# Seven half-size block products for 20 tile pairs of the first channel-mixing product, with weight sums on GpSimd

## Chip, cores and metric

The kernel runs on one NeuronCore of a Trainium2 chip. The metric is the device time of one execution in microseconds. TensorE is the matmul engine, VectorE (DVE), ScalarE (ACT) and GpSimd (POOL) compute beside it, and SyncE (SP) issues most DMAs.

## What is computed

One decoder block on 512 tokens of width 1024: a mixing sub-layer (a recurrence and a dilated attention, merged by gates) and a channel sub-layer. The change lies in the channel sub-layer:

```python
h = modulate(rms_norm(x, g_pre_ffn[i]), shift_f, scale_f)
u, gt = jnp.split(h @ w_ffn_in[i], 2, axis=-1)
f = (jax.nn.silu(u) * gt) @ w_ffn_out[i]
x = x + gate_f[:, None, :] * rms_norm(f, g_post_ffn[i])
```

The products are wanted nearly in fp32. Every operand is therefore split into a rounded part (hi) and a residual (lo), and every block product is three matmuls: hi x hi, hi x lo, lo x hi.

## The kernel before

A helper `split` (L110 to L112) casts a tile to its high part on ScalarE (L111) and subtracts it on VectorE for the residual (L112). `weights(i)` loads one weight tile of 128x1024 fp32 (512 KB) on SP's queue into one of three slots called raw, and splits it; the high and low tiles have two slots each in the pool wp, or come from another pool that is passed in. `mm3` issues the three matmuls of a block. All this is traced at high priority, so that a scheduler puts it ahead of the work that is traced beside it, in each engine's queue; within a queue the order is then fixed.

The end of the kernel, in order. **Merge**: eight channel tiles of the merged mixers, split into mh and ml. **Output product** (`natural_gemm`, tokens on the partitions): eight k tiles; the first four are taken for all four token tiles in turn, the last four ("tail") are held back and taken token tile by token tile, so that each tile's accumulation ends as early as possible. **Norm** (`post_norm`, and the lines behind it): for each token tile the residual x2 and the normalised row xn. After two token tiles their rows are transposed on TensorE (L915), evacuated with scale and shift (hf, L921 and L923) and split into h2h and h2l, 256 columns at a time.

**First channel-mixing product**: 22 pairs of weight tiles, u (for SiLU) and g. For a tile, eight k blocks of 128x128 are multiplied with h2 over all 512 tokens: `ffn_mm`, 24 matmuls of 512 columns. The first two pairs are computed in token halves (256 columns) while the second half of h2 is still being made; their weights lie in wp and in the pool ow. The other 20 pairs follow. For each pair `ffn_evac` applies SiLU (L945), multiplies by g (L946) and splits the result into fh and fl for the second product. After pair 8 the last eight columns of the modulation (`ada_col`, a weight tile times the condition vector on VectorE, L168) are loaded on POOL's queue and `ada_comb` forms comb_f. **Second channel-mixing product**: `natural_gemm` over 22 k tiles, with the norm and the output behind it.

There are eight PSUM banks of 512 columns, in four groups that rotate: mm (3), b (2), c (2), y (1). A pair now takes two banks of mm.

Of the kernel before, what the change touches and what calls it, by code (L numbers as in the profile page):

```python
# [18 lines left out]
P = 128  # L19
D = 1024  # L20
# [64 lines left out]
def block_kernel(ctx, tc, x, vec, cst, cst2, cst3, crow, ada, win0, lora, wts, wa, out):  # L85
# [21 lines left out]
    def mm(o, l, r, start, stop):  # L107
        return nc.tensor.matmul(o, l, r, start=start, stop=stop)  # L108

    def split(hi, lo, src):  # L110
        A.copy(hi, src)  # L111
        V.tensor_tensor(out=lo, in0=src, in1=r32(hi), op=ALU.subtract)  # L112

    def weights(i, pool=None, src=None, n=1024):
        with tc.high_priority():
            raw = wp.tile([P, 1024], F32, tag="raw", name=nm("raw"), bufs=3)[:, 0:n]
            nc.sync.dma_start(raw, wts[i] if src is None else src)
            if pool is None:
# [43 lines left out]
        V.reciprocal(t, t)  # L162
        return t

    def ada_col(pool, tag, bufs, i, eng):
        aw = pool.tile([P, D], F32, tag=tag, name=nm("aw"), bufs=bufs)
# [671 lines left out]
    with ExitStack() as phY:  # L838
        yp = phY.enter_context(tc.tile_pool(name="yp", bufs=1))
        for ct in range(KT):  # L840
# [11 lines left out]
            V.tensor_tensor(out=gb, in0=gb, in1=ya, op=ALU.add)  # L852
            split(mh[:, ct, :], ml[:, ct, :], gb)
    phZ.close()
    phH = ExitStack()
    h2p = phH.enter_context(tc.tile_pool(name="h2p", bufs=1, side="right"))
    h2h = h2p.tile([P, KT, S], F32R, name="h2h")
    h2l = h2p.tile([P, KT, S], F32R, name="h2l")

    op_ = phO.enter_context(tc.tile_pool(name="op", bufs=1))  # L860
    op_.tile([P, 80], F32, name="pad_o")
    ow = phO.enter_context(tc.tile_pool(name="ow", bufs=6))

    def natural_gemm(w0, nk, ah, al, tail, pool):
        accs = [[bank("mm"), bank("mm")], [bank("mm"), bank("c")], [bank("c"), bank("y")], [bank("b"), bank("b")]]

        def part(k, wh, wl, i, hs=(0, 1)):
            t = slice(i * P, (i + 1) * P)
            for (l, w, first, last) in ((ah, wh, True, False), (al, wh, False, False), (ah, wl, False, True)):
                for h in hs:  # L870
                    mm(accs[i][h], l[:, k, t], w[:, h * 512:(h + 1) * 512], k == 0 and first, k == nk - 1 and last)
        for k in range(nk - tail):
            wh, wl = weights(w0 + k)
            for i in range(NTT):
                part(k, wh, wl, i)
# [24 lines left out]
    xns = []  # L900
    for i, acc in natural_gemm(W_OUT, KT, mh, ml, 4, ow):
        post_norm(op_, acc, comb_m, x2[i], x2[i])
        s1 = op_.tile([P, 1], F32, tag="s1", name=nm("s1"), bufs=2)
        xn = op_.tile([P, D], F32, tag="xn", name=nm("xn"), bufs=2)
        A.activation(xn, x2[i], AF.Square, accum_out=s1)
        rs = rstd_of(op_, s1, D, 1, eps_rms)
        V.tensor_scalar(out=xn, in0=x2[i], scalar1=rs, scalar2=None, op0=ALU.mult)
        xns.append(xn)
        if i % 2 == 1:
            t0 = (i - 1) * P  # L910
            for j2 in range(KT // 2):
                pt = bank("c" if i == 1 else "b")
                for jj in range(2):
                    for ii in range(2):
                        nc.tensor.transpose(pt[:, (2 * jj + ii) * P:(2 * jj + ii + 1) * P],  # L915
                                            xns[i - 1 + ii][:, (2 * j2 + jj) * P:(2 * j2 + jj + 1) * P], ident)
                for jj in range(2):
                    j = 2 * j2 + jj
                    hf = op_.tile([P, 256], F32, tag="hf2", name=nm("hf2"), bufs=2)
                    if jj == 0:  # L920
                        A.activation(hf, pt[:, 0:256], AF.Identity, scale=modf[:, 8 + j:9 + j], bias=modf[:, j:j + 1])  # L921
                    else:
                        V.tensor_scalar(out=hf, in0=pt[:, 256:512], scalar1=modf[:, 8 + j:9 + j], scalar2=modf[:, j:j + 1], op0=ALU.mult, op1=ALU.add)  # L923
# [133 lines left out]
```

## Time and profile before

| | us |
|---|---|
| median of 3 runs | 995.48 |
| lowest and highest | 989.5, 1003.88 |
| profiled execution | 990.31 |
| span from first to last instruction of it | 988.5 |
| TensorE busy (matmul) | 945.8, 96% |
| VectorE busy | 577.2, 58% |
| ScalarE busy | 396.1, 40% |
| GpSimd busy | 41.9, 4% |

The mean granted clock of TensorE is 0.98 of full speed. The profile puts a group's count, busy time, the mean of one, and the idle time of its engine in front of it side by side; a timeline row has a start, a length and what the engine waited for. Matmuls overlap: one of 512 columns shows 0.39 us, but the next starts sooner, so a stream is read from the starts.

### The profile page before, as it was taken

Reading aid. Unit: us, or ns where it says so; the run is one execution under the profiler, and the core shown is the slowest. Engines: PE = TensorE matmul, PEld = TensorE weight load, DVE = VectorE, ACT = ScalarE, POOL = GpSimd, SP = SyncE. Lnnn points to the kernel's source line nnn. Section 1 sums busy time; section 2 is a strip of 40 time slices with the busy share of each in tenths; the row PEclk is TensorE's granted clock in tenths of the full one; section 3 lists DMA queues with packets and bytes.
Section 4 is the critical chain, followed back from the end, with each engine's and each line's share of the span. In section 5 each row is a group of like instructions: output and inputs, shape, how many; then the busy total and the mean of one; then the engine's idle time right before and its main releaser. Section 6 shows DMA issues by size and latency. Waiting matters only on the chain.

```text
span 988.5 us, 13834 instructions
## 1 busy us (share of the span) xinstructions
PE 945.8 (96%) x5468; PEld 757.5 (77%) x5468; DVE 577.2 (58%) x1050; ACT 396.1 (40%) x633; POOL 41.9 (4%) x85
## 2 busy tenths in 40 slices
PE   6999989999999999998999899999999999999997
PEld 4887767777867876786788678988888888888885
DVE  6986799955699975375655576573333333412234
ACT  7568443433586232332382246532323232321223
POOL 0000000100010010010000100010000000000000
PEclk9999999999999987999899999999999999999999
DMA  9753435423231322139326863163332323233322
GB/s 369 280 164 117 157 122 173 136 97 116 100 125 63 102 91 86 34 139 277 122 93 219 292 223 96 42 232 97 99 119 95 106 87 107 86 107 89 103 86 86
DMA packets 47170, 131.73 MB, mean 133 GB/s; under 512 B 11249, under 2 KB 12033, under 8 KB 47106
## 3 DMA queue, kind: packets, MB, share of 16 engines
q1 hardware_dynamic: 27792, 96.74, 30.0%
q10 hardware_dynamic: 13970, 16.27, 5.2%
q0 software_dynamic: 5344, 17.84, 4.8%
q8 instruction: 43, 0.70, 0.3%
q14 instruction: 21, 0.17, 0.1%
HBM read 116.14 MB, written 14.69 MB: 132 GB/s over the span
## 4 chain that ended last, share of the span: by engine, by line
PE 74%; DVE 10%; issue 8%; DMA 5%; ACT 2%; ACTq 1%; POOL 0%; SPq 0%; DVEq 0%; POOLq 0%
PE ps L108 72%; DVE lo L112 1%; DVE fP L526 1%; DMA k<-d_k 1%; DVE fT L530 1%; DMA d_ya<-t 1%; DMA aw<-in_ada_dram 1%; DVE T L534 1%; DMA x<-in_x_dram 1%; DMA gb<-d_gate 1%; ACT xg L490 1%; DVE aw L168 1%; PE ps L308 1%; DVE Sg L486 0%; DMA VN<-d_v 0%
## 5 line engine op out<-in xcount | busy, mean ns | idle before, releaser
L111 ACT CAST hi<-raw 128x1024 fp32r<-128x1024 f32 (+1 forms) x130 | 133.0, 1025 | 346.0 <-PE ps L108 276.0
L112 DVE TENSOR_TENSOR lo<-raw,hi 128x1024 fp32r<-128x1024 f32 (+1 forms) x130 | 154.6, 1189 | 167.6 <-ACT hi L111 161.6
L108 PE MATMUL ps<-hl,hi 128*128 128x512 f32 x432 | 175.1, 405 | 0.0
L108 PE MATMUL ps<-hh,lo 128*128 128x512 f32 x432 | 174.3, 403 | 0.8 <-DVE lo L112 0.8
L108 PE MATMUL ps<-hh,hi 128*128 128x512 f32 x432 | 172.7, 409 | 0.2
L108 PE MATMUL ps<-h2h,hi 128*128 128x512 f32 (+1 forms) x352 | 133.5, 381 | 0.7 <-ACT u L945 0.7
L108 PE MATMUL ps<-h2l,hi 128*128 128x512 f32 (+1 forms) x352 | 133.5, 380 | 0.2 <-DVE h2l L112 0.2
L108 PE MATMUL ps<-h2h,lo 128*128 128x512 f32 (+1 forms) x352 | 133.2, 379 | 0.0
L108 PEld LDWEIGHTS ps<-hh,lo 128*128 128x128 f32 x432 | 82.8, 192 | 18.5 <-DVE lo L112 1.2
L108 PEld LDWEIGHTS ps<-hh,hi 128*128 128x128 f32 x432 | 82.6, 191 | 18.6 <-issue 1.3
L108 PEld LDWEIGHTS ps<-hl,hi 128*128 128x128 f32 x432 | 82.9, 192 | 16.7 <-issue 0.2
L108 PEld LDWEIGHTS ps<-h2h,hi 128*128 128x128 f32 x352 | 66.0, 188 | 13.7 <-ACT u L945 0.9
L108 PEld LDWEIGHTS ps<-h2l,hi 128*128 128x128 f32 x352 | 66.1, 188 | 13.1 <-DVE h2l L112 0.4
L108 PEld LDWEIGHTS ps<-h2h,lo 128*128 128x128 f32 x352 | 66.1, 188 | 12.5
L168 DVE SCALAR_TENSOR_TENSOR aw<-aw,silur 128x1024 f32<-128x1024 f32 x48 | 58.2, 1219 | 9.4 <-DMA aw<-in_ada_dram 9.3
L946 DVE TENSOR_TENSOR u<-u,ps 128x512 f32<-128x512 f32 x22 | 15.0, 687 | 66.6 <-PE ps L108 59.0
L108 PE MATMUL ps<-hi,fh 128*128 128x512 f32 x144 | 44.4, 389 | 0.0
L108 PE MATMUL ps<-lo,fh 128*128 128x512 f32 x144 | 44.4, 389 | 0.0
L108 PE MATMUL ps<-hi,fl 128*128 128x512 f32 x144 | 44.3, 389 | 0.0
L108 PEld LDWEIGHTS ps<-hi,fh 128*128 128x128 f32 x144 | 27.0, 188 | 5.7
L108 PEld LDWEIGHTS ps<-hi,fl 128*128 128x128 f32 x144 | 27.0, 188 | 5.6
L108 PEld LDWEIGHTS ps<-lo,fh 128*128 128x128 f32 x144 | 27.0, 188 | 5.6
(292 smaller groups left out, 1372.9 us busy)
## 6 DMA issues: line engine op xcount, KB each, us to landing
raw<-in_wts_dram SPq DMA_DIRECT2D x124, 512.0 KB, 3.6
aw<-in_ada_dram SPq DMA_DIRECT2D x40, 512.0 KB, 4.3
d_gate<-t POOLq DMA_DIRECT2D x16, 256.0 KB, 3.0
aw<-in_ada_dram POOLq DMA_DIRECT2D x8, 512.0 KB, 4.7
raw<-in_win_dram SPq DMA_DIRECT2D x8, 384.0 KB, 6.7
raw<-in_wa_dram SPq DMA_DIRECT2D x8, 384.0 KB, 3.2
x<-in_x_dram SPq DMA_DIRECT2D x4, 512.0 KB, 5.7
t<-d_gate ACTq DMA_DIRECT2D x8, 256.0 KB, 2.8
```

The lines of the kernel that those rows point to most:

```text
L108: return nc.tensor.matmul(o, l, r, start=start, stop=stop)
L111: A.copy(hi, src)
L112: V.tensor_tensor(out=lo, in0=src, in1=r32(hi), op=ALU.subtract)
L168: V.scalar_tensor_tensor(out=aw, in0=aw, scalar=1.0, in1=silur, op0=ALU.mult, op1=ALU.mult, accum_out=modv[:, i:i + 1])
L308: nc.tensor.transpose(pt[:, i * P:(i + 1) * P], xt[i][:, j * P:(j + 1) * P], ident)
L490: A.copy(xg[64 * e + 32 * b:64 * e + 32 * b + 32, :, p * NCH:(p + 1) * NCH], sgm[32 * b:32 * b + 32, e, :, 32 * b:32 * b + 32].rearrange(" ...
L526: V.tensor_tensor(out=pv, in0=fU[:, t + 1 + a:t + 1 + b, t, None].to_broadcast([P, b - a, m]), in1=fT[:, t, None, 0:m].to_broadcast([P, b ...
L530: V.tensor_tensor(out=rows, in0=rows, in1=pv, op=ALU.add)
L534: V.transpose(t1a[:, e], fT[64 * e:64 * e + 32].rearrange("k a b -> k b a"))
L946: V.tensor_tensor(out=u, in0=u, in1=pg, op=ALU.mult)
```

## The change

For 20 of the 22 pairs the product of a pair is written as a product of 2x2 blocks. The weight pair is cut into u and g (128 columns each) and into two halves of the inner dimension (four k tiles each); the activations h2 are cut into those halves and into two halves of the tokens (256 each). Instead of eight block products there are seven (Winograd's form): `prod` multiplies one half tile of weights, or of a sum of weight blocks, with one of seven activation blocks, 12 matmuls of 256 columns. The activation blocks are 11, 21 and 22 of h2 and four sums t1 to t4, made and split once behind the first two pairs. The weight sums are made for each pair on GpSimd (four additions of 128x512 into s31 and s24) and then split; the pair needs 3.5 splits of 1024 instead of two. The products are combined from PSUM on VectorE into rr; SiLU then goes to a PSUM bank, and the pair's result is kept in fp32 (ff).

Around it: the output product holds back three k tiles instead of four, and ow has three slots instead of six; h2 is kept unsplit (hf_0, hf_1) and split in blocks of 1024 after four evacuations; ff is split into hi and lo only in the second product (`acts`), two tiles of it ahead of time; the modulation columns are loaded during pairs 3 to 10 on SP's queue into space of ff, and comb_f is formed at pair 12. `natural_gemm` takes a function for its activations. `post_norm` has one junk tile (jk) instead of two and three tiles pn instead of four.

The diff, cut to its core:

```diff
...
+    om = phO.enter_context(tc.tile_pool(name="om", bufs=1))
+    comb_m = om.tile([P, D], F32, name="comb_m")
+    op_ = phO.enter_context(tc.tile_pool(name="op", bufs=1))
+    op_.tile([P, 80], F32, name="pad_o")
+    ow = phO.enter_context(tc.tile_pool(name="ow", bufs=3))
+    phM = ExitStack()
+    mp = phM.enter_context(tc.tile_pool(name="mp", bufs=1))
...
-    h2h = h2p.tile([P, KT, S], F32R, name="h2h")
-    h2l = h2p.tile([P, KT, S], F32R, name="h2l")
-    op_ = phO.enter_context(tc.tile_pool(name="op", bufs=1))
-    op_.tile([P, 80], F32, name="pad_o")
-    ow = phO.enter_context(tc.tile_pool(name="ow", bufs=6))
-    def natural_gemm(w0, nk, ah, al, tail, pool):
+    HB = {n: ((h2q if n == "12" else h2p).tile([P, 1024], F32R, name=f"h2h_{n}"),
+              (h2q if n == "12" else h2p).tile([P, 1024], F32R, name=f"h2l_{n}"))
+          for n in ("12", "11", "21", "22", "t1", "t2", "t3", "t4")}
+    h2q.tile([P, 48], F32, name="pad_h")
...
-            jk = pool.tile([P, 512], F32, tag="jk", name=nm("jk"), bufs=2)
+            jk = pool.tile([P, 512], F32, tag="jk", name=nm("jk"), bufs=1)
...
-            u = pool.tile([P, 512], F32, tag="pn", name=nm("pn"), bufs=4)
+            u = pool.tile([P, 512], F32, tag="pn", name=nm("pn"), bufs=3)
...
-    for i, acc in natural_gemm(W_OUT, KT, mh, ml, 4, ow):
+    xns, hfs = [], []
+    for i, acc in natural_gemm(W_OUT, KT, lambda k: (mh[:, k, :], ml[:, k, :]), 3, ow):
...
+            th = i // 2
+            if th == 0:
+                hf = op_.tile([P, KT, 256], F32, name="hf_0")
+            else:
+                phM.close()
+                tp = phM.enter_context(tc.tile_pool(name="tp", bufs=1))
+                hf = tp.tile([P, KT, 256], F32, name="hf_1")
+            hfs.append(hf)
...
+                if j2 % 2 == 1:
+                    hb = HB[f"{1 + j2 // 2}{1 + th}"]
+                    split(hb[0], hb[1], hf[:, 2 * j2 - 2:2 * j2 + 2, :].rearrange("p a b -> p (a b)"))
...
+    def prod(ps, w, ks, b, start=True, stop=True):
         wh, wl = w
-        for k in range(KT):
+        for n, k in enumerate(ks):
             ws = slice(k * P, (k + 1) * P)
-            mm3(ps[:, t], wh[:, ws], wl[:, ws], h2h[:, k, t], h2l[:, k, t], k == 0, k == KT - 1)
+            t = slice(n * 256, (n + 1) * 256)
+            mm3(ps, wh[:, ws], wl[:, ws], HB[b][0][:, t], HB[b][1][:, t], start and n == 0, stop and n == 3)
...
+            ps = b0[q][:, half * 256:half * 256 + 256]
+            prod(ps, w0[q], K0, f"1{half + 1}", True, False)
+            prod(ps, w0[q], K1, f"2{half + 1}", False, True)
...
+    blk = {f"{r + 1}{t + 1}": hfs[t][:, 4 * r:4 * r + 4, :].rearrange("p a b -> p (a b)") for r in range(2) for t in range(2)}
+    ts = {n: tp.tile([P, 1024], F32, tag="ts", name=nm("ts"), bufs=3) for n in ("t1", "t3", "t2")}
+    V.tensor_tensor(out=ts["t1"], in0=blk["11"], in1=blk["12"], op=ALU.subtract)
+    split(*HB["t1"], ts["t1"])
+    V.tensor_tensor(out=ts["t3"], in0=blk["22"], in1=blk["12"], op=ALU.subtract)
+    split(*HB["t3"], ts["t3"])
+    V.scalar_tensor_tensor(out=ts["t2"], in0=ts["t1"], scalar=-1.0, in1=blk["22"], op0=ALU.mult, op1=ALU.subtract)
+    split(*HB["t2"], ts["t2"])
+    ts["t4"] = tp.tile([P, 1024], F32, tag="ts", name=nm("ts"), bufs=3)
+    V.scalar_tensor_tensor(out=ts["t4"], in0=ts["t2"], scalar=-1.0, in1=blk["21"], op0=ALU.mult, op1=ALU.subtract)
+    split(*HB["t4"], ts["t4"])
+    phM.close()
...
+    ff = [fp.tile([P, S], F32, name=f"ff_{i}") for i in range(NF - 4)]
+    fe = [fp.tile([P, 2 * S], F32, name=f"fe_{i}") for i in range(2)]
+    ff += [fe[i // 2][:, i % 2 * S:(i % 2 + 1) * S] for i in range(4)]
...
+    L, R = slice(0, 512), slice(512, 1024)
+    for i in range(2, NF):
+        ru, rg = raw_of(W_FI + 2 * i), raw_of(W_FI + 2 * i + 1)
+        wa_ = ssplit(ru, 1024, wp, ("hi", "lo"), 2)
+        with tc.high_priority():
+            s31 = sp.tile([P, 1024], F32, tag="s31", name=nm("s31"), bufs=1)
+            s24 = sp.tile([P, 1024], F32, tag="s24", name=nm("s24"), bufs=1)
+            G.tensor_tensor(out=s31[:, L], in0=rg[:, L], in1=ru[:, L], op=ALU.add)
+            G.tensor_tensor(out=s31[:, R], in0=rg[:, L], in1=rg[:, R], op=ALU.add)
+            G.tensor_tensor(out=s24[:, L], in0=s31[:, R], in1=ru[:, L], op=ALU.add)
+            G.tensor_tensor(out=s24[:, R], in0=s24[:, L], in1=ru[:, R], op=ALU.add)
+        wb_ = ssplit(s31, 1024, sp, ("sh", "sl"), 3)
+        wc_ = ssplit(s24, 1024, sp, ("sh", "sl"), 3)
+        wd_ = ssplit(rg[:, R], 512, sp, ("dh", "dl"), 1)
+        p1, p26 = bank("b")[:, 0:256], bank("c").rearrange("p (a b) -> p a b", a=2)
+        p75 = bank("mm").rearrange("p (a b) -> p a b", a=2)
+        p43 = bank("mm" if i % 2 else "y").rearrange("p (a b) -> p a b", a=2)
+        prod(p1, wa_, K0, "11")
+        s1 = sp.tile([P, 256], F32, tag="p1", name=nm("p1"), bufs=1)
+        A.copy(s1, p1)
+        prod(p26[:, 0], wa_, K1, "21")
+        prod(p75[:, 0], wb_, K0, "t3")
+        prod(p75[:, 1], wb_, K1, "t1")
+        prod(p26[:, 1], wc_, K0, "t2")
+        rr = sp.tile([P, 4, 256], F32, tag="rr", name=nm("rr"), bufs=1)
+        V.tensor_tensor(out=rr[:, 0:4:3], in0=p26, in1=s1[:, None, :].to_broadcast([P, 2, 256]), op=ALU.add)
+        V.tensor_tensor(out=rr[:, 1:3], in0=p75, in1=rr[:, 3, None, :].to_broadcast([P, 2, 256]), op=ALU.add)
+        V.tensor_tensor(out=rr[:, 3], in0=p75[:, 1], in1=rr[:, 1], op=ALU.add)
+        prod(p43[:, 1], wc_, K1, "22")
+        prod(p43[:, 0], wd_, K0, "t4")
+        V.tensor_tensor(out=rr[:, 1:3], in0=p43, in1=rr[:, 1:3], op=ALU.add)
+        A.activation(p26, rr[:, 0:4:2], AF.Silu)
+        V.scalar_tensor_tensor(out=ff[i].rearrange("p (a b) -> p a b", a=2), in0=rr[:, 1:4:2], scalar=-1.0, in1=p26,
+                               op0=ALU.mult, op1=ALU.mult)
+        if 3 <= i < 11:
+            ada_col(None, None, 0, 37 + i, nc.sync, fe[i % 2])
+        if i == 12:
+            ada_comb(5, V_PF, comb_f, "b")
+    def acts(k):
+        if k < 2:
+            hi, lo = HB["12"][k][:, 0:S], HB["12"][k][:, S:2 * S]
...
+            hi = fs.tile([P, S], F32R, tag="fh", name=nm("fh"), bufs=6)
+            lo = fs.tile([P, S], F32R, tag="fl", name=nm("fl"), bufs=6)
+        with tc.high_priority():
+            split(hi, lo, ff[k])
+        return hi, lo
...
-    for i in range(2, NF):
-        pu, pg = bank("mm"), bank("mm")
-        ffn_mm(pu, weights(W_FI + 2 * i), slice(0, S))
-        ffn_mm(pg, weights(W_FI + 2 * i + 1), slice(0, S))
-        ffn_evac(i, pu, pg)
-        if i == 8:
-            for q in range(8):
-                ada_col(ep_, "aw2", 3, 40 + q, G)
-            ada_comb(5, V_PF, comb_f, "b")
...
```

## Rows read from the trace of the kernel before

**Rows 1.** Stretches: busy us (instructions) by engine; then clock, DMA share, GB/s
```profile
650.00:700.00 50.00, 50.00 (x222) 41.39 (x221) 24.94 (x35) 15.40 (x20) 2.15 (x4) 1.00 0.46 147
...
900.00:950.00 50.00, 50.00 (x222) 41.42 (x221) 12.40 (x11) 11.48 (x12) 0.00 (x0) 1.00 0.34 104
```

**Rows 2.** All waits of TensorE from 570 us to the end: us, times, longest
```profile
PE ps L108 <- DVE gb L851: 1.9, 3, 1.2
PE ps L108 <- ACT u L945: 0.7, 1, 0.7
PE ps L108 <- DVE h2l L112: 0.2, 1, 0.2
```

**Rows 3.** Timeline of TensorE (start us, length): first and last of 960, and the next
```profile
643.98 0.50 PE L108 MATMUL ps<-h2h,hi 128*128 128x512 f32 x1 [0.69 <-ACT u L945]
...
861.66 0.39 PE L108 MATMUL ps<-h2h,lo 128*128 128x512 f32 x1
861.89 0.62 PE L108 MATMUL ps<-hi,fh 128*128 128x512 f32 x2
```

**Rows 4.** Timeline of TensorE, 256 columns: first and last of 48
```profile
637.38 0.28 PE L108 MATMUL ps<-h2h,hx 128*128 128x256 f32 x1
...
643.02 0.28 PE L108 MATMUL ps<-h2h,lx 128*128 128x256 f32 x1
```

**Rows 5.** Groups by line and shape from 600 us: busy us, mean ns | idle before
```profile
L112 DVE TENSOR_TENSOR lo<-raw,hi 128x1024 fp32r<-128x1024 f32 x58 | 71.0, 1225 | 136.1 <-ACT hi L111 134.2
...
L111 ACT CAST hi<-raw 128x1024 fp32r<-128x1024 f32 x58 | 61.1, 1054 | 221.5 <-PE ps L108 213.7 <-issue 7.8
...
L112 DVE TENSOR_TENSOR fl<-u,fh 128x512 fp32r<-128x512 f32 x22 | 15.1, 685 | 0.1
...
L946 DVE TENSOR_TENSOR u<-u,ps 128x512 f32<-128x512 f32 x22 | 15.0, 687 | 66.6 <-PE ps L108 59.0 <-ACT u L945 4.2 <-PE ps L175 3.4
...
L111 ACT CAST fh<-u 128x512 fp32r<-128x512 f32 x22 | 13.6, 621 | 3.3 <-DVE u L946 3.3
...
L945 ACT ACTIVATE u<-ps 128x512 f32<-128x512 f32 x22 | 12.8, 585 | 3.5 <-PE ps L108 3.5
...
L112 DVE TENSOR_TENSOR h2l<-hf,h2h 128x256 fp32r<-128x256 f32 x16 | 6.6, 420 | 1.6 <-ACT h2h L111 0.9
...
L108 PEld LDWEIGHTS ps<-h2h,hx 128*128 128x128 f32 x32 | 6.1, 191 | 0.0
...
L896 DVE SCALAR_TENSOR_TENSOR x<-pn,rstd,x 128x512 f32<-128x512 f32 x8 | 5.7, 748 | 0.1
...
L921 ACT ACTIVATE hf<-ps,modf 128x256 f32<-128x256 f32 x8 | 4.5, 564 | 2.2 <-PE ps L915 2.2
```

**Rows 6.** Groups of POOL: the memset nearest in shape
```profile
L699 POOL MEMSET VN<- 128x512 f32 x3 | 1.5, 536 | 3.2 <-DVE t L230 3.2
```

**Rows 7.** DMA issues from 650 to 860 us: KB each, median us to landing
```profile
raw<-in_wts_dram SPq DMA_DIRECT2D x39, 512.0 KB, 3.5
aw<-in_ada_dram POOLq DMA_DIRECT2D x4, 512.0 KB, 5.0
```

**Rows 8.** Timelines: tails of tiles 1 and 2, first pairs; last, VectorE
```profile
598.61 0.62 PE L108 MATMUL ps<-hx,mh 128*128 128x512 f32 x2
...
604.05 0.62 PE L108 MATMUL ps<-hx,mh 128*128 128x512 f32 x2
...
616.62 0.28 PE L108 MATMUL ps<-h2h,hi 128*128 128x256 f32 x1
...
612.79 0.76 DVE L907 TENSOR_SCALAR xn<-x,rstd 128x1024 f32<-128x1024 f32 x1
```

**Rows 9.** Stretches as in rows 1, around TensorE's slow clock
```profile
315.00:320.00 5.00, 3.61 (x19) 2.62 (x19) 3.95 (x15) 4.87 (x9) 0.00 (x0) 1.00 0.00 0
...
355.00:360.00 5.00, 4.41 (x55) 3.25 (x55) 4.91 (x5) 1.96 (x4) 1.44 (x2) 1.00 0.07 24
...
365.00:370.00 5.00, 5.00 (x64) 3.92 (x63) 1.58 (x4) 2.27 (x4) 0.00 (x0) 0.50 0.02 3
```

More of the change, by code (lines that the diff above doesn't have):

```diff
@@ L163, in rstd_of, with ada_col @@
         return t
-    def ada_col(pool, tag, bufs, i, eng):
-        aw = pool.tile([P, D], F32, tag=tag, name=nm("aw"), bufs=bufs)
+    def ada_col(pool, tag, bufs, i, eng, aw=None):
+        if aw is None:
+            aw = pool.tile([P, D], F32, tag=tag, name=nm("aw"), bufs=bufs)
         eng.dma_start(aw, ada[i])
@@ L854, in block_kernel, with natural_gemm, part @@
     phZ.close()
+    h2q = ctx.enter_context(tc.tile_pool(name="h2q", bufs=1, side="right"))
     phH = ExitStack()
     h2p = phH.enter_context(tc.tile_pool(name="h2p", bufs=1, side="right"))
-    h2h = h2p.tile([P, KT, S], F32R, name="h2h")
-    h2l = h2p.tile([P, KT, S], F32R, name="h2l")
-    op_ = phO.enter_context(tc.tile_pool(name="op", bufs=1))
-    op_.tile([P, 80], F32, name="pad_o")
-    ow = phO.enter_context(tc.tile_pool(name="ow", bufs=6))
-    def natural_gemm(w0, nk, ah, al, tail, pool):
+    HB = {n: ((h2q if n == "12" else h2p).tile([P, 1024], F32R, name=f"h2h_{n}"),
+              (h2q if n == "12" else h2p).tile([P, 1024], F32R, name=f"h2l_{n}"))
+          for n in ("12", "11", "21", "22", "t1", "t2", "t3", "t4")}
+    h2q.tile([P, 48], F32, name="pad_h")
+    def natural_gemm(w0, nk, acts, tail, pool):
         accs = [[bank("mm"), bank("mm")], [bank("mm"), bank("c")], [bank("c"), bank("y")], [bank("b"), bank("b")]]
-        def part(k, wh, wl, i, hs=(0, 1)):
+        def part(k, act, wh, wl, i, hs=(0, 1)):
             t = slice(i * P, (i + 1) * P)
+            ah, al = act
             for (l, w, first, last) in ((ah, wh, True, False), (al, wh, False, False), (ah, wl, False, True)):
                 for h in hs:
-                    mm(accs[i][h], l[:, k, t], w[:, h * 512:(h + 1) * 512], k == 0 and first, k == nk - 1 and last)
+                    mm(accs[i][h], l[:, t], w[:, h * 512:(h + 1) * 512], k == 0 and first, k == nk - 1 and last)
         for k in range(nk - tail):
             wh, wl = weights(w0 + k)
+            act = acts(k)
             for i in range(NTT):
-                part(k, wh, wl, i)
-        ws = [weights(w0 + k, pool) for k in range(nk - tail, nk)]
+                part(k, act, wh, wl, i)
+        ws = [(k, acts(k), *weights(w0 + k, pool)) for k in range(nk - tail, nk)]
         for i in range(NTT):
             for hs in ((0, 1),) if i < NTT - 1 else ((0,), (1,)):
-                for k in range(nk - tail, nk):
-                    part(k, *ws[k - nk + tail], i, hs)
+                for w in ws:
+                    part(*w, i, hs)
             yield i, accs[i]
@@ L963, in block_kernel @@
-    for i, acc in natural_gemm(W_FO, NF, fh, fl, 4, fo):
-        ot = ep_.tile([P, D], F32, tag="aw2", name=nm("ot"), bufs=3)
+    ff = [fp.tile([P, S], F32, name=f"ff_{i}") for i in range(NF - 4)]
+    fe = [fp.tile([P, 2 * S], F32, name=f"fe_{i}") for i in range(2)]
+    ff += [fe[i // 2][:, i % 2 * S:(i % 2 + 1) * S] for i in range(4)]
+    phS = ExitStack()
+    sp = phS.enter_context(tc.tile_pool(name="sp", bufs=1))
+    for i in range(2):
+        uf = sp.tile([P, S], F32, tag="u", name=nm("u"), bufs=1)
+        A.activation(uf, b0[2 * i], AF.Silu)
+        V.tensor_tensor(out=ff[i], in0=uf, in1=b0[2 * i + 1], op=ALU.mult)
@@ new lines, in raw_of, with ssplit @@
+    def raw_of(i):
+        with tc.high_priority():
+            raw = wp.tile([P, 1024], F32, tag="raw", name=nm("raw"), bufs=3)
+            nc.sync.dma_start(raw, wts[i])
+        return raw
+    def ssplit(src, n, pool, tags, bufs):
+        with tc.high_priority():
+            hi = pool.tile([P, n], F32R, tag=tags[0], name=nm(tags[0]), bufs=bufs)
+            lo = pool.tile([P, n], F32R, tag=tags[1], name=nm(tags[1]), bufs=bufs)
+            split(hi, lo, src)
+        return hi, lo
+    L, R = slice(0, 512), slice(512, 1024)
@@ new lines, in acts @@
+    def acts(k):
+        if k < 2:
+            hi, lo = HB["12"][k][:, 0:S], HB["12"][k][:, S:2 * S]
+        else:
+            hi = fs.tile([P, S], F32R, tag="fh", name=nm("fh"), bufs=6)
+            lo = fs.tile([P, S], F32R, tag="fl", name=nm("fl"), bufs=6)
+        with tc.high_priority():
+            split(hi, lo, ff[k])
+        return hi, lo
+    phS.close()
+    fs = ctx.enter_context(tc.tile_pool(name="fs", bufs=1))
+    phH.close()
+    pf = ctx.enter_context(tc.tile_pool(name="pf", bufs=1, side="right"))
@@ L965, in block_kernel @@
+    pf.tile([P, 80], F32, name="pad_f")
+    fo = ctx.enter_context(tc.tile_pool(name="fo", bufs=4, side="right"))
+    ep_ = ctx.enter_context(tc.tile_pool(name="ep", bufs=1))
+    for i, acc in natural_gemm(W_FO, NF, acts, 4, fo):
+        ot = ep_.tile([P, D], F32, tag="ot", name=nm("ot"), bufs=3)
         post_norm(ep_, acc, comb_f, x2[i], ot, out[i * P:(i + 1) * P, :])
```

25 lines of the change are left out of this document (4 added, 21 removed).

## Prediction

> **What bounds the kernel now.** I read the profile from the whole to the stage that is changed. The table by stretch comes first: from 650 to 950 us TensorE is busy all the time at a granted clock of 1.00, while VectorE is busy 50% at first and 25% later, ScalarE 31% to 23%, and GpSimd issues a few DMAs [rows 1]. So the stage of the pairs is bound by the matmul stream alone. The waits of TensorE from 570 us to the end confirm it: 2.8 us in all, 1.9 of them in the merge, and 0.7 us at the entry to the first changed pair [rows 2]. Next the timeline of TensorE gives the stage its exact price: the twenty pairs run from 643.98 to 861.89 us, 217.9 us for 960 matmuls of 512 columns, 0.227 us from start to start [rows 3]. Last I looked for matmuls of the changed form. They exist: the first two pairs are computed in token halves, and from 637.38 to 643.02 us 48 matmuls of 256 columns start 0.120 us apart (5.64 us over 47 steps) [rows 4], each with its own weight load. A weight load shows 191 ns [rows 5], longer than that spacing, and yet the stream keeps 0.120 us: the loads overlap.
>
> **What the seven products remove.** A pair takes 16 blocks of 3 matmuls of 512 columns, 48 x 0.227 = 10.89 us. After the change it takes 7 products x 4 k tiles x 3 matmuls = 84 matmuls of 256 columns, 84 x 0.120 = 10.08 us. The columns fall by an eighth (24,576 to 21,504), but the time only by 7.5%, since 2 x 0.120 is 0.240 and not 0.227: 0.013 us of every matmul does not depend on the columns, and there are 36 more of them. Twenty pairs: 217.9 - 201.6 = **16.3 us saved**, if TensorE never waits. The Trainium skill prices it otherwise: "TensorE: Matmul & The Clock Gate", section "Wait — 56ns, not 53.3ns?", gives columns over 2.4 GHz plus about 2.5 ns, by which the estimate is 84 x 0.109 against 48 x 0.216, 1.2 us a pair and 24 us in all. The trace disagrees at both sizes (0.120 and 0.227), and I go by the trace.
>
> **What it adds per pair beside TensorE.** VectorE: three residuals of 1024 (1.225 us) and one of 512 (0.685) are 4.36; three combinations of 512 out of PSUM at 0.687, one of 256 at 0.42 and the last at 0.75 are 3.23; 7.6 us together, against 3.8 before [rows 5]. The eight modulation columns add 1.22 us to eight pairs, as before. ScalarE: three casts of 1024 at 1.054, one of 512 at 0.621, the copy of p1 at most 0.56, SiLU 0.585; 4.9 us [rows 5]. Both fit under 10.08, so I cost them at nothing; the cover is the double buffering, since a pair's weights can be prepared while the pair before is multiplied (two slots for the u halves, three for the sums), and the PSUM banks come round no sooner than about a pair later. If that cover goes, VectorE's spare time is only 10.08 - 7.6 = 2.5 us a pair.
>
> **GpSimd** gets four additions of 128x512 with two inputs. No such instruction runs before; POOL only clears tiles and issues DMAs. Below, an addition can't be expected under a memset of 128x512, 0.536 us [rows 6]; above, I take three such passes, two reads and one write, 1.61 us. Nearest is the middle, since reads may partly overlap: 1.07 us, 4.3 us a pair (2.1 to 6.4).
>
> What decides is a ring, not this busy time. There are three raw slots and two loads a pair. The raw u tile is read by the last sum, so the g tile of the next pair may find its slot only after that sum; it lands 3.5 us later [rows 7], and only then can the next four sums start. The ring costs 3.5 + 4.3 = 7.8 us a pair, 9.9 at the upper bound: below 10.08 in both cases. It becomes the bound when a sum takes more than (10.08 - 3.5)/4 = 1.64 us. In the eight pairs with a modulation column the DMA may take 5.0 [rows 7], with sums of 1.07 still 9.3. So the steady pairs cost 10.08.
>
> **What it moves.** The modulation loads go from POOL's queue to SP's, behind raw loads that are issued earlier; each waits for a buffer used two pairs before, so SP should not stand still: 0. POOL's two DMAs for comb_f now stand in the queue of the sums; the second waits for the first one's landing and stops the sums of one pair for some 2 us, inside the spare time of the ring: 0. The split of the activations (0.621 and 0.685 us) moves into the last product, where a k step lasts 24 x 0.227 = 5.44 us and needs 1.68 us of ScalarE and 1.91 of VectorE: hidden, 0. One junk buffer and three instead of four product buffers in the norm: in-order work on one engine, 0 to 0.5 us.
>
> **The way in, first part.** The output product keeps three k tiles back instead of four, so a token tile's accumulation takes 18 x 0.227 = 4.08 us at the end instead of 5.44. Tile 0 is done at 598.61 and tile 1 at 604.05 now [rows 8]; with one k step more in the common part and shorter tails, tile 1 is done at 598.61 + 2 x 4.08 = 606.8. From there its normalised row takes until 612.79 + 0.76, 9.5 us [rows 8], so 616.3. The product itself ends about 614.9, as the 16 transposes can no longer be threaded into it. Then four evacuations must pass before the first split of 1024: transposes 0.6, two on ScalarE at 0.56 with VectorE's a step behind, about 1.7, the cast 1.05: the high half is there at 619.7, and the product of the first pairs starts there rather than at 616.62 [rows 8]. That is 3.1 us late; the transposes are by then out of the way. Lost: **3 us**, 0 to 6.
>
> **Second part.** Pair 2's sums write into memory that the first pairs' weights hold until their last matmul. From there: two sums 2.1, cast 1.05, residual 1.23, some 0.8 for handing over and the two SiLUs in front: 5.2 us, of which the two products on the raw u weights cover 24 x 0.120 = 2.9. Lost: **2.3 us**, 0.4 (if TensorE takes the t4 product first, which needs no sum) to 6 (if the residuals of t1 to t4, eight VectorE instructions of 1.2 us, stand in front). The 0.7 us at this place now [rows 2] goes, as p1 uses another bank.
>
> **Sum.** 990.3 - 16.3 - 0.7 + 3 + 2.3 = 978.6 us, on the scale of the profiled execution, 1.2% below it. That execution lies 5 us under the median shown (995.48, runs from 989.5 to 1003.9); on the median's scale it is 984. I name 981. A difference of 2%, some 20 us, is about what a measurement of this kernel can tell from none, and the largest saving here, 17.0 us with no stall, lies under it.
>
> **The rivals.**
> - *GpSimd and VectorE exclude each other* (slower). If each sum waits for a whole residual that is running, it takes 1.07 + 1.23 = 2.3 us and the ring 3.5 + 9.2 = 12.7: 20 x 2.6 more, 1031 us. It decides from 2.04 us a sum on (ring 11.65, time 1010). For it: both engines now read SBUF for most of a pair, 4.36 and 4.3 of 10.08 us. Against it: ring waits leave gaps, in which the residuals can run. No row shows either. The Trainium skill speaks for it: "SBUF — State Buffer", section "Who interferes with whom", says that a VectorE instruction with two SBUF inputs and a GpSimd instruction reading SBUF hold a shared port one at a time, and "GPSIMD Engine Reference", section 3.1, gives 4497 ns for an addition of 2048, an estimate of 1.12 us here; by that price alone the ring would be 8.0 and the sum the same. Chance 0.13.
> - *The ring binds a little.* Sums of 1.64 to 2.04 us; at 1.8 the ring is 10.7, 20 x 0.62 = 12 us: 991. Chance 0.16.
> - *The way in costs more.* TensorE idles 4 to 8 us near 615 us, and the clock falls. The trace shows 0.50 at 365 to 370 us after a stretch in which TensorE was busy 4.41 of 5 us; but a stretch with 3.61 of 5 kept 1.00 [rows 9]. Ten matmul us at 1.2 instead of 2.4 GHz cost 5 to 10 us: 987. Chance 0.13.
> - *The overhead of a matmul vanishes* and the whole eighth is gained, by the page's price: 24 us instead of 16.3, 971. Against it stand 48 starts in a row at 0.120 us. Chance 0.05.
> - *The forecast*, TensorE bound at 10.08 a pair: chance 0.53, own range 974 to 990.
>
> **Numbers.** Slower by over 2% is the first rival, 0.13. Faster by over 2% is the fourth and a bare edge of the forecast, 0.07. Within 2% is the rest, 0.80. The range leaves out the first and the fourth rival: 973 from the saving without any stall, 1003 from the second rival's upper part on the median's scale.
>
> **What would show it.** Right: matmuls of 256 columns 0.120 us apart through all pairs, a pair every 10.1 us, the stage some 202 us long, TensorE's waits confined to the two places on the way in. Wrong: TensorE waiting in every pair for a residual or a cast of the sums, POOL additions over 1.6 us, residuals much longer than 1.23 us, or a clock under 1.00 behind 615 us.

## Result, and the profile after

The changed kernel takes 1037.62 us (median of 4 runs, 1034.49 to 1041.37) against 993.38 for the kernel before (4 runs beside it): a ratio of 1.043, 95% interval 1.034 to 1.0519. It is slower. The profiled executions differ by as much: spans of 1035.3 and 988.5 us, **46.8 us** more. The forecast was 981 us, its range 973 to 1003: both wrong, and on the wrong side.

The busy times hardly hint at it. The page's line of busy time, share and instructions by engine shows TensorE as long at work as before, though the seven products should have taken some 16 us off its work by the forecast. So TensorE stands still in the added time, and part of its work runs slowly.

```profile
PE 946.7 (91%) x6188; PEld 789.8 (76%) x6188; DVE 708.1 (68%) x1166; ACT 435.1 (42%) x685; POOL 185.0 (18%) x157
```

Where it lies is read from the starts on TensorE's timeline (start us, length, and in brackets the idle time before it and its releaser): first the first pairs' product, then the first block matmul of the first of the 20 pairs, one of pair 4 (pairs are counted from 0, so the first of the 20 is pair 2), three of successive pairs near the middle, and the first matmul of the second product that waits.

```profile
619.58 0.80 PE L108 MATMUL ps<-h2h,hi 128*128 128x256 f32 x2
...
646.04 0.28 PE L108 MATMUL ps<-h2h,hi 128*128 128x256 f32 x1
...
685.22 0.55 PE L108 MATMUL ps<-h2h,hi 128*128 128x256 f32 x1 [9.38 <-DVE ff L1032]
...
723.79 0.28 PE L108 MATMUL ps<-h2h,hi 128*128 128x256 f32 x1
...
733.68 0.28 PE L108 MATMUL ps<-h2h,hi 128*128 128x256 f32 x1
...
743.57 0.28 PE L108 MATMUL ps<-h2h,hi 128*128 128x256 f32 x1
...
907.49 0.93 PE L108 MATMUL ps<-hi,h2h 128*128 128x512 f32 x3 [2.78 <-DVE rr L1027]
```

The stage of the pairs begins at 646.04 instead of 643.98 [rows 3], 2.1 us late. It ends at 904.31 and lasts 258.3 us instead of 217.9: **40.4 us**, most of the loss, and 12.9 us a pair where 10.08 were forecast. The second product adds 4.4, of which 2.78 are the wait at 907.49. These make 46.9, the whole difference but for rounding. Where no pair waits (723.79, 733.68, 743.57) a pair takes 9.89 us. So the matmuls are as cheap as promised, and something stops them.

The waits of TensorE from 560 us to the end (us in total, times, longest) name it:

```profile
PE ps L108 <- DVE dl L112: 19.6, 11, 2.0
PE ps L108 <- DVE ff L1032: 14.4, 3, 9.4
PE ps L108 <- DVE rr L1027: 4.2, 2, 2.8
PE ps L108 <- ACT sh L111: 3.1, 2, 2.3
PE ps L930 <- DVE xn L915: 3.0, 1, 3.0
PE ps L108 <- DVE sl L112: 1.9, 6, 0.5
```

Before there were 2.8 us of waits in this part [rows 2]; now eleven pairs wait for dl, the residual of the last weight block. The groups by line and shape (busy us, mean ns of one; then idle before) show why it is late:

```profile
L112 DVE TENSOR_TENSOR sl<-s,sh 128x1024 fp32r<-128x1024 f32 x40 | 70.3, 1757 | 17.9 <-ACT sh L111 17.8
...
L1007 POOL TENSOR_TENSOR s<-raw,raw 128x512 f32<-128x512 f32 x20 | 41.3, 2066 | 174.1 <-PE ps L108 86.4 <-DMA raw<-in_wts_dram 80.1 <-DVE lo L112 6.0
...
L1010 POOL TENSOR_TENSOR s<-s,raw 128x512 f32<-128x512 f32 x20 | 41.0, 2050 | 1.6
...
L1008 POOL TENSOR_TENSOR s<-raw 128x512 f32<-128x512 f32 x20 | 39.0, 1948 | 0.0
...
L112 DVE TENSOR_TENSOR dl<-raw,dh 128x512 fp32r<-128x512 f32 x20 | 29.7, 1486 | 1.5 <-ACT dh L111 1.5
...
L1009 POOL TENSOR_TENSOR s<-s,raw 128x512 f32<-128x512 f32 x20 | 26.8, 1340 | 5.0 <-DVE sl L112 3.7
```

The sums take 7.4 us a pair (the four means added), not 4.3. And VectorE's residuals, whose form and size did not change, became longer: sl takes 1.757 where the same subtraction took 1.225, and dl 1.486 where 512 columns took 0.685 [rows 5]. Both engines are slower when both run. The timelines of one pair show how. GpSimd:

```profile
845.93 2.15 POOL L1007 TENSOR_TENSOR s<-raw,raw 128x512 f32<-128x512 f32 x1 [4.80 <-DMA raw<-in_wts_dram]
848.04 2.27 POOL L1008 TENSOR_TENSOR s<-raw 128x512 f32<-128x512 f32 x1
850.38 1.30 POOL L1009 TENSOR_TENSOR s<-s,raw 128x512 f32<-128x512 f32 x1
851.76 2.12 POOL L1010 TENSOR_TENSOR s<-s,raw 128x512 f32<-128x512 f32 x1
```

and VectorE beside it:

```profile
845.70 1.23 DVE L112 TENSOR_TENSOR lo<-raw,hi 128x1024 fp32r<-128x1024 f32 x1 [2.07 <-ACT hi L111]
846.84 2.32 DVE L112 TENSOR_TENSOR sl<-s,sh 128x1024 fp32r<-128x1024 f32 x1
849.08 0.68 DVE L1025 TENSOR_TENSOR rr<-ps,p 128x512 f32<-128x512 f32 x1
...
850.52 0.42 DVE L1027 TENSOR_TENSOR rr<-ps,rr 128x256 f32<-128x256 f32 x1
851.43 1.34 DVE L112 TENSOR_TENSOR sl<-s,sh 128x1024 fp32r<-128x1024 f32 x1 [0.49 <-ACT sh L111]
852.69 1.74 DVE L112 TENSOR_TENSOR dl<-raw,dh 128x512 fp32r<-128x512 f32 x1
```

Read them by their ends: lo ends at 846.93, the first sum at 848.08, sl at 849.16, the second sum at 850.31. Four instructions that would overlap in pairs end one after another, 1.1 to 1.2 us apart: they take turns, and each shows its own turn and the one it waited for. It is not one tile that both want: that sl reads a sum of the pair before, while the first two sums read raw tiles alone. VectorE's reads of PSUM (849.08 to 850.94) keep their 0.68, 0.69 and 0.42 us beside the second and the third sum, and the third, which starts beside the last of them, takes 1.30 us. Then it begins again: the fourth sum (851.76) ends 1.1 us after sl, and dl 0.55 us after that sum.

The chain that ended last, taken over 845 to 872 us (start us, us, what), shows the loop this closes. One round:

```profile
841.70 4.07 DMA raw<-in_wts_dram
...
845.93 2.15 POOL s L1007
848.08 2.24 POOL s L1008
...
850.34 1.06 ACT sh L111
...
851.43 0.06 DVE sl L112
851.49 1.20 issue
852.69 1.75 DVE dl L112
...
854.46 3.90 DMA raw<-in_wts_dram
...
867.11 4.37 DMA raw<-in_wts_dram
```

A load starts every 12.7 us (841.70, 854.46, 867.11). In the round stand a load, **two** sums, a cast, the residual sl, and dl, which is behind sl in VectorE's queue and is the last reader of the raw g tile. When dl is done, the next load gets the slot. TensorE isn't in the round at all; it meets it as "waits for dl".

A second round runs beside it, which the chain doesn't show because it is a little shorter. The fourth sum is the last reader of the raw u tile. When it ends (853.88 us), the next u load is issued; the g load, which the next sums wait for, stands behind that one in SyncE's queue:

```profile
853.91 0.33 SPq L989 DMA_DIRECT2D raw<-in_wts_dram  x1
...
854.46 0.33 SPq L989 DMA_DIRECT2D raw<-in_wts_dram  x1
```

Where the slot is free, a g load follows its u load after 0.42 us (the runs with residuals from PSUM, below); here that would be 854.33, only 0.13 us before dl lets it go. From the end of one fourth sum to the end of the next (841.13 to 853.88) this round holds 4.80 us for the loads and 7.95 for **four** sums.

The first sum of a pair starts at 646.35 us in the first pair and at 884.52 in the last: 19 intervals of 12.54 us on average, 12.0 to 13.2 from 757 us on and 7.7 to 15.5 before. The rounds set the pace even where TensorE has fallen behind, by its waits for ff, and catches up at 9.89 us a pair, from 723.79 to 753.47: the first sums start at 731.70, 743.47 and 757.28, 11.8 and 13.8 apart, and from 762 us on TensorE waits again in every pair but the last.

### The profile page after: what moved, and what is told of

It reads as the page before. It is cut to its first block, busy times and chain, and to the rows that moved or that the text cites. A ratio compares the mean times of both kernels' runs of the same rounds, so it can differ in the third digit from the quotient of the medians.

```text
span 1035.3 us, 15666 instructions
## 1 busy us (share of the span) xinstructions
PE 946.7 (91%) x6188; PEld 789.8 (76%) x6188; DVE 708.1 (68%) x1166; ACT 435.1 (42%) x685; POOL 185.0 (18%) x157
## 4 chain that ended last, share of the span: by engine, by line
PE 49%; DVE 17%; DMA 11%; issue 11%; POOL 7%; ACT 4%; POOLq 0%; ACTq 0%; SPq 0%; DVEq 0%
PE ps L108 47%; DMA raw<-in_wts_dram 6%; POOL s L1008 3%; POOL s L1007 3%; DVE dl L112 2%; DVE lo L112 2%; DVE fP L527 1%; DVE fT L531 1%; ACT sh L111 1%; DVE sl L112 1%; DMA VN<-d_v 1%; DMA aw<-in_ada_dram 1%; DVE T L535 1%; DMA d_ya<-t 1%; DVE aw L169 1%
## 5 line engine op out<-in xcount | busy, mean ns | idle before, releaser
L112 DVE TENSOR_TENSOR sl<-s,sh 128x1024 fp32r<-128x1024 f32 x40 | 70.3, 1757 | 17.9 <-ACT sh L111 17.8
L111 ACT CAST sh<-s 128x1024 fp32r<-128x1024 f32 x40 | 42.0, 1050 | 76.7 <-POOL s L1008 61.2
L108 PE MATMUL ps<-h2h_t,sh 128*128 128x256 f32 x240 | 69.8, 291 | 4.5 <-ACT sh L111 3.1
L108 PE MATMUL ps<-h2h_t,sl 128*128 128x256 f32 x240 | 70.0, 292 | 1.9 <-DVE sl L112 1.9
L108 PE MATMUL ps<-h2h,hi 128*128 128x256 f32 x192 | 57.0, 299 | 14.4 <-DVE ff L1032 14.4
L108 PE MATMUL ps<-h2l_t,sh 128*128 128x256 f32 x240 | 69.3, 289 | 0.0
L108 PE MATMUL ps<-h2l,hi 128*128 128x256 f32 x192 | 56.3, 295 | 0.2 <-DVE h2l L112 0.2
L108 PE MATMUL ps<-h2h,lo 128*128 128x256 f32 x192 | 55.9, 292 | 0.0
L108 PEld LDWEIGHTS ps<-h2h_t,sh 128*128 128x128 f32 x240 | 47.7, 199 | 5.1 <-ACT sh L111 5.1
L108 PEld LDWEIGHTS ps<-h2h_t,sl 128*128 128x128 f32 x240 | 47.6, 199 | 3.2 <-DVE sl L112 3.1
```

## Experiments

The theory from here on: VectorE's two-input instructions on SBUF and GpSimd's sums hold each other up, and a ring of raw slots turns that into the pace ("port"). Its rivals: too few slots, whatever the sums cost ("slots"); and something else in the stage, such as the modulation columns or the clock.

**Two more raw slots.** Block 12 of h2 is dead behind the first pairs; its 8 KB become two slots for the g tiles.

```diff
-            raw = wp.tile([P, 1024], F32, tag="raw", name=nm("raw"), bufs=3)
+            raw = qtile(nm("rawg"), F32) if i % 2 else wp.tile([P, 1024], F32, tag="raw", name=nm("raw"), bufs=3)
```

> Changed kernel, with two more slots for raw weights: the g tiles are loaded into the 8 KB that hold activation block 12 until the first two pairs are done. Theory 'ring' (each pair's loads wait for the last sum of the pair before, 4.8 us of load plus 7.8 us of sums): the loads run ahead, the sums no longer wait for them, pairs every 9.9 to 10.5 us, the stage 200 to 210 us, time 978 to 992. Rival 'port' (GpSimd and VectorE hold each other up, whatever the slots): sums and residuals stay stretched and lie denser, VectorE's 7.6 plus up to 4.8 us a pair, pairs every 11 to 12.4 us, time 1005 to 1030. Rival 'slow sums' (GpSimd takes 2 us by itself): as ring, since 7.8 is under 9.9.

Measured: 1015.87 us, ratio 1.022 (1.0167 to 1.0274), span 1012.1; the stage 236.9 us. It is 22 us better and still slower than before, as the rival "port" said, and not as "ring" did. A pair in the steady part takes 11.2 us, on TensorE's timeline:

```profile
806.36 0.28 PE L108 MATMUL ps<-h2h,hi 128*128 128x256 f32 x1
...
817.53 0.28 PE L108 MATMUL ps<-h2h,hi 128*128 128x256 f32 x1
```

Both rounds are still there, with two slots for g alone. The load issue, the first sum and the residuals in the timelines of SyncE, GpSimd and VectorE:

```profile
827.42 0.33 SPq L991 DMA_DIRECT2D rawg<-in_wts_dram  x1
...
831.53 1.62 POOL L1009 TENSOR_TENSOR s<-rawg,raw 128x512 f32<-128x512 f32 x1 [4.69 <-DVE lo L112]
...
835.54 1.35 DVE L112 TENSOR_TENSOR sl<-s,sh 128x1024 fp32r<-128x1024 f32 x1 [1.76 <-ACT sh L111]
836.80 1.77 DVE L112 TENSOR_TENSOR dl<-rawg,dh 128x512 fp32r<-128x512 f32 x1
```

From the load at 827.42 to the end of dl at 838.57 are 11.15 us. The load at 827.42 takes the slot that the dl just before it has freed (827.40). That dl is the pair before's, but it stands behind this pair's first sl in VectorE's queue; so two slots for g do not break the round. The u tiles have three slots now and are loaded pairs ahead, but such a load still waits for a fourth sum (end 826.84, issue 826.87) and stands in front of the g load; so the second round isn't broken either. The sums became shorter (the first two 1.619 and 1.574 instead of 2.066 and 1.948), because they now meet VectorE's reads of PSUM more often.

**The sums on VectorE.** Nothing else changes; three slots.

```diff
-            G.tensor_tensor(out=s31[:, L], in0=rg[:, L], in1=ru[:, L], op=ALU.add)
+            V.tensor_tensor(out=s31[:, L], in0=rg[:, L], in1=ru[:, L], op=ALU.add)
...
```

> Changed kernel, with the four sums of a pair on VectorE instead of GpSimd, nothing else moved. Ring: 4.8 + 4 x 0.69 = 7.6 us, no longer the bound; VectorE has 7.6 + 2.8 = 10.4 us a pair, a little over TensorE's 9.9, and 11.6 in the eight pairs with a modulation column; residuals back at 1.23 and 0.69 us; time 985 to 1000. Rival 'queue order' (the residual of the last product stands too late in VectorE's queue, whatever GpSimd does): TensorE still waits 1 to 2 us for it in most pairs, time 1010 or more.

Measured: 991.06 us, ratio 0.9989 (0.9951 to 1.0028), span 989.5; the stage 215.6 us. That is 45.8 us less span than with the sums on GpSimd, though VectorE now does more. Groups by line (busy us, mean ns):

```profile
L112 DVE TENSOR_TENSOR sl<-s,sh 128x1024 fp32r<-128x1024 f32 x40 | 48.7, 1220 | 3.2 <-ACT sh L111 3.2
...
L1007 DVE TENSOR_TENSOR s<-raw,raw 128x512 f32<-128x512 f32 x20 | 13.7, 686 | 4.0 <-DMA raw<-in_wts_dram 3.1 <-PE ps L108 0.9
```

The residual is back at 1.220 and a sum costs 0.686. The price is that VectorE is busy 137.9 of the 150 us from 700 to 850 us, and TensorE waits for it here and there (rr 5.8 us, ff 4.6, modv 2.8).

**A residual with one input.** The sums stay on GpSimd and the slots are three; in the 20 pairs the low part of the weights comes from an instruction of the same size that reads one SBUF tile only, so this kernel leaves the residuals out.

```diff
-            split(hi, lo, src)
+            A.copy(hi, src)
+            V.tensor_scalar(out=lo, in0=r32(hi), scalar1=0.0, scalar2=None, op0=ALU.mult, op1=ALU.add,
+                            accum_out=sp.tile([P, 1], F32, tag="ac", name=nm("ac"), bufs=2))
```

> Changed kernel, with the sums on GpSimd as they are, but the residuals of the 20 pairs' weights written by a VectorE instruction with one input and an accumulator (zeros times the high part, so the residuals are left out of the computation). It reads one tile of SBUF instead of two. Port: all sums 1.3 us, the ring 4.8 + 5.2 = 10.0, time 980 to 995. Slow sums: the sums stay at 2.0 us and the ring at 12.6, time 1030 to 1040.

Measured (one run): 988.24 us, span 986.5; the stage 212.8 us; a pair takes 9.92 (809.00 to 818.92 us). Groups by line:

```profile
L997 DVE TENSOR_SCALAR_CACHE_REDUCE sl<-sh 128x1024 fp32r<-128x1024 f32 x40 | 48.6, 1216 | 41.8 <-ACT sh L996 41.8
...
L1010 POOL TENSOR_TENSOR s<-raw 128x512 f32<-128x512 f32 x20 | 27.8, 1390 | 0.0
L1012 POOL TENSOR_TENSOR s<-s,raw 128x512 f32<-128x512 f32 x20 | 27.6, 1380 | 1.6
...
L1009 POOL TENSOR_TENSOR s<-raw,raw 128x512 f32<-128x512 f32 x20 | 26.0, 1299 | 169.6 <-PE ps L108 85.6 <-DMA raw<-in_wts_dram 75.9 <-ACT hi L996 4.8
```

VectorE is occupied as long per residual as when undisturbed (1.216 against 1.220), with the same slots and columns, and GpSimd does the same sums; the second SBUF input is gone. The sums fall from 1.34–2.07 to 1.30–1.39, so it is the second input that stretches them, and not that VectorE works at all. The pairs come to TensorE's own pace and the span falls by 48.8 us. One thing more has changed, though: the instruction no longer reads the raw tile, so dl is no longer the slot's last reader, and the first round is gone altogether. The second round never held sl or dl, and what has changed in it is its sums: from 805.47 to 815.51 us, the issues of two u loads, it takes 10.04 us, with 5.32 for the four sums instead of 7.95. So the stretched sums alone are enough for the slow pace.

**Both remedies.** Slots and the sums on VectorE together.

> Both: two more raw slots and the sums on VectorE. If the ring was all that the slots cut, and it does not bind with the sums on VectorE, this is as fast as sums on VectorE alone, within 3 us (VectorE bound, 10.4 us a pair). If the slots matter on their own, 5 us or more faster.

Measured: 989.63 us, ratio 0.9928 (0.9885 to 0.9971), span 986.5; the stage 214.6. Beside the run with the sums on VectorE alone, two more slots are worth 1 us of the stage and 3 of the span. So "slots" falls as a cause of its own: without the contention they are hardly needed.

**The columns out of the stage.** Slots as in the first run, and the eight modulation columns moved to k steps 3 to 10 of the second product, where comb_f is then formed by DMAs.

```diff
-        if 3 <= i < 11:
-            ada_col(None, None, 0, 37 + i, nc.sync, fe[i % 2])
...
+        if 3 <= k < 11:
+            ada_col(wp, "raw", 3, 37 + k, nc.sync)
```

> Two more raw slots, sums on GpSimd, and the eight modulation columns moved out of pairs 3 to 10 into the second product (k steps 3 to 10, comb_f then formed by DMAs alone). If VectorE's queue in the first pairs is what the columns cost, the uneven first pairs go and the pairs keep the 11.2 us that they have in steady state with two more slots: the stage 20 x 11.2 = 224 us instead of 237, time 1000 to 1008. If the columns are hidden, time as with two more slots alone, 1011 to 1018.

Measured: 1016.36 us, ratio 1.0254 (1.0159 to 1.0349), span 1010.3. The expected gain didn't come. Inside the stage it did: 227.6 us, 9 less, at 11.2 a pair from the fourth pair on, and the long waits for ff are gone (0.3 us). But the stage starts 2.8 us later than with the slots alone, and TensorE then waits 4.4 us for rr at the entry of the second product. With two more slots the columns cost what they put into early pairs, and 7.5 of those 9 us come back at the seams (2.8 ahead of the stage, 4.7 behind it).

**All three together.** Sums on VectorE, two more slots, columns in the second product.

> Two more raw slots, sums on VectorE, modulation columns in the second product. VectorE has 10.4 us a pair from the first pair on instead of 11.6 in eight of them: eight times 1.2 less, 6 to 10 us under slots and sums on VectorE alone (989.6), time 978 to 984. If the columns were hidden there: 987 to 992.

Measured: **976.72 us, ratio 0.9855 (0.9777 to 0.9932)**, span 975.5; the stage 205.2 us. This is just under the forecast of 978 to 984. The interval lies under 1, so it is faster than the kernel before; whether by 2% the interval leaves open. From 700 to 850 us (width; busy time of TensorE, its weight loads, VectorE, ScalarE, GpSimd; clock, DMA share, GB/s):

```profile
700.00:850.00 150.00, 149.35 (x1243) 147.30 (x1244) 139.34 (x194) 67.21 (x90) 0.00 (x0) 1.00 0.29 102
```

TensorE is the bound again, with VectorE close behind it at 93%. This is the seven-product form at nearly its own price: 205.2 against 197.8 by 20 pairs of 9.89.

**Residuals from PSUM.** A way to keep GpSimd: ScalarE copies the high part of the sums' and the last block's weights to a PSUM bank, and VectorE subtracts that; one SBUF input again, and nothing left out. With slots and moved columns:

```diff
+            A.copy(hi, src)
+            for h in range(0, n, 512):
+                hp = bank("b")
+                A.copy(hp, r32(hi[:, h:h + 512]))
+                V.tensor_tensor(out=lo[:, h:h + 512], in0=src[:, h:h + 512], in1=hp, op=ALU.subtract)
```

> Two more raw slots, modulation columns in the second product, sums on GpSimd, and for the split of the sums and of the last half g tile the high part is also copied to a PSUM bank, from which VectorE takes it for the residual: five of the seven residual halves of a pair then read one tile of SBUF. Port: sums 1.3 to 1.6 us, VectorE 8 us a pair, ScalarE 8, TensorE bound at 9.9, time 975 to 984. Slow sums: sums stay at 1.6 to 2 us. A third possibility: the copies to two banks that p1 shares make ScalarE and VectorE wait for each other, pairs 10.5 to 11.5 us, time 988 to 1010.

Measured: 991.75 us, ratio 0.9969 (0.9927 to 1.0012), span 990.7; the stage 215.8 us, pairs 10.1 to 10.5. Groups by line:

```profile
L1009 DVE TENSOR_TENSOR sl<-s,ps 128x512 fp32r<-128x512 f32 x80 | 52.8, 681 | 6.8 <-ACT ps L1008 4.6
...
L1022 POOL TENSOR_TENSOR s<-s,raw 128x512 f32<-128x512 f32 x20 | 26.0, 1299 | 1.6
```

The contention is gone here too (sums 1.29 to 1.32), by another road than in the one-input run. But no engine is full (ScalarE 104.5, VectorE 105.2, GpSimd 74.7 of 150 us), TensorE waits 14 times for sl, and it lies 15 us behind the best version. What sets 10.3 instead of 9.9 is the second round, in which GpSimd waits 104 us for the g loads. SyncE's issues of a u load, a g load and the next u load:

```profile
774.99 0.33 SPq L991 DMA_DIRECT2D raw<-in_wts_dram  x1
775.41 0.38 SPq L991 DMA_DIRECT2D rawg<-in_wts_dram  x1
...
785.30 0.33 SPq L991 DMA_DIRECT2D raw<-in_wts_dram  x1
```

A fourth sum ends at 774.97. Only then is a later pair's u load issued, and the g load that the next sums wait for follows 0.42 us behind it, though dl has freed its slot at 775.15. The next first sum starts at 779.95, and the four undisturbed sums end at 785.27: 10.3 us. The third possibility gave about the right time, by another mechanism. A kernel that issues the g load ahead of the u load was not tried.

**The same alone**, with three slots and the columns where they were:

> Changed kernel with only the residuals of the sums and of the last half g tile taken from PSUM as above, three raw slots, columns where they were. Port: four sums 5.4 to 6.4 instead of 7.8 us, ring 10.2 to 11.2, time 990 to 1008. Slow sums: 1030 to 1040, or more by the added copies.

Measured (one run): 1018.4 us, span 1015.6; the stage 240.5, pairs of 10 to 11.5 and some of 13. Missed by 10 us. The first sum still takes 1.838, the others 1.33 to 1.36: it starts beside lo, the u tile's residual, and the columns, which still read two SBUF tiles. TensorE waits 20.4 us for sl. The residuals of the sums no longer hold the sums up, but the second round is left, with sums that are still partly stretched: 11.5 and 11.1 us between the u loads issued at 836.92, 848.43 and 859.53 us, 6.2 and 6.1 of them for the four sums. So with three slots and the columns the gain of this road is under half (19.7 us of span against 48.8 with one input).

## Why the prediction was wrong, point by point

**TensorE's price: right.** 0.120 us a matmul gave 10.08 a pair; undisturbed pairs take 9.89, 0.118 each. So the saving exists (20.1 us by 9.89), and the best version shows 12.7 us of it in the stage (205.2 against 217.9).

**The way in: right in time.** The wait for xn ends at 615.75 (forecast 616.3), the first pairs' product starts at 619.58 (619.7), pair 2 waits 3.1 us for sh (2.3). The clock of the rival did fall: behind the waits for xn and hf the granted clock was 0.58 from 615 to 620 us and 0.73 from 620 to 625, and behind those for sh 0.50 (the level of 1.2 GHz) from 655 to 660. Its price did not come, as the stage begins only 2.1 us late. Behind that, 96 matmuls from 646.04 to 663.72 us take 17.7 us, where 11.3 and the waits of 3.1 make 14.4; whether the other 3.3 cost anything in the end isn't shown.

**VectorE and ScalarE cover their work: right in sum, wrong in order.** VectorE is busy 113.6 of 150 us from 700 to 850 in the changed kernel, so it was never full. "Both fit under 10.08, so I cost them at nothing" overlooked that work which fits can still stand in front of the instruction that frees a slot: dl behind sl.

**The price of a sum: wrong, and this began it.** The step was "Nearest is the middle", 1.07 us and so 4.3 a pair. A sum takes 1.29 to 1.32 us by itself (the run with residuals from PSUM and two more slots) and 1.34 to 2.07 on average in the changed kernel, 7.95 for the four in the steady part. At 1.30 alone little would have happened: the first round with undisturbed terms is 4.1 + 2 x 1.30 + 1.06 + 1.22 + 0.69 = 9.7 us (an estimate), and the second took 10.0 and 10.3 us in the two runs with undisturbed sums, about TensorE's own 9.9. The second half of the price, taking turns with VectorE, was the rival with 0.13. Its argument against itself, "ring waits leave gaps, in which the residuals can run", failed: in the trace lo and sl run just when the sums do, since the same landed loads and casts release both. On this the Trainium skill, "SBUF — State Buffer", section "Who interferes with whom", which the prediction set beside the rival, agrees with every trace here: turns with two SBUF inputs (sums up to 2.37 us), none with one input or with one from PSUM (1.30). It should have carried more than 0.13.

**The ring: the right loop with both terms too small, and another beside it.** The forecast's ring was a load and four sums, 3.5 + 4.3 = 7.8. It is in the trace as the second round, with 4.80 + 7.95 = 12.75. The load term is longer since a u load is issued ahead of the g load (0.42 to 0.55 us) and g, with two of 512 KB under way, lands 4.1 us after its issue instead of 3.5. The slot that waits for the last sum is u's; the g load waits behind u's. The rival's 3.5 + 9.2 = 12.7 has this loop and the right mechanism, and its 1031 us came close to 1037.6; that its sums were 1.25 too long and its load 1.3 too short is luck. Beside it stands the round of the chain, of other parts: load 4.07, two sums 4.39, cast 1.06, sl 1.26, dl 1.75, 12.5 in all and 12.76 with small gaps. A cast and two residuals in a ring were in no term of mine. A kernel with dl earlier in the queue wasn't tried; the second round, 0.13 us shorter, would have left it little to gain (an estimate).

**The columns in eight pairs: wrong by their place.** Costed at nothing, "still 9.3". TensorE's 14.4 us of waits for ff, 9.38 at once, lie among the pairs with a column. The 9.38 are a wait for the ff of pair 2, which stands in VectorE's queue behind a residual of pair 5's sums (683.16 us). The column instruction itself, with two SBUF inputs, takes 1.576 instead of 1.219 (the mean of the 40 others). Inside the stage they cost 9 us with the slots in place.

**The clock.** In 680 to 690 us TensorE was busy 4.79 of 10 us, behind the 9.38 us wait, at a granted clock of 0.50; over the stage the mean is 0.93.

```profile
680.00:690.00 10.00, 4.79 (x22) 4.82 (x23) 5.64 (x8) 3.01 (x5) 5.44 (x4) 0.50 0.34 127
```

TensorE is busy 217.5 of the 258.3 us, 19.7 more than 20 times 9.89: its matmuls fill part of the gaps by being slow. In the steady part that costs nothing of its own, since TensorE is in neither round: the first sums lie 12.6 us apart at a granted clock of 0.87 (845.5 to 858.2 us), and 11.8 and 13.8 where it is 1.00 (731.7 to 757.3 us). For the pairs before, it isn't shown. A wait table alone would understate the loss (40.8 us of waits in a stage that is 60.5 longer than its price).

**The second product: missed.** PSUM banks were costed at nothing; the entry waits 2.78 us for the last pair's combination to give its bank back, behind a residual in VectorE's queue.

## What to carry to other kernels

Before moving elementwise work to GpSimd, look at what VectorE does in the same microseconds: two-input work on SBUF beside it makes both take turns, and then the move can cost more than doing the work on VectorE (0.69 us here against 1.3 to 2.1). Price a ring of buffers from its last reader: the load, what stands ahead of that load in its own queue, plus everything that stands ahead of the releasing instruction in its engine's queue, not only the instructions that use the tile. And a cut in matmul columns by an eighth is worth 7.5 to 9% when the matmuls become narrower.

## What the runs showed of the hardware

An addition of 128x512 fp32 takes 1.30 us on GpSimd undisturbed, 0.686 on VectorE; GpSimd takes 1.9 times as long even when nothing runs beside it that delays it. The turns are whole instructions: one of 1024 columns on VectorE delays a sum by up to 1.1 us, and a sum delays the residual as much, shown as a longer instruction and not as a wait, so that no wait view names it. Of two loads of 512 KB issued together, the second stands in the chain with 3.9 to 4.4 us, where the median was 3.5 before [rows 7].
